# A hybrid decoder step: GpSimd's two-input operations move to VectorE, its scaling of probabilities to ScalarE

## The chip, the cores and the metric

The kernel runs on one core of a Trainium2 chip. The core has five engines with a queue of instructions each, run in order: TensorE (PE in the profile, with PEld for its weight loads), VectorE (DVE), ScalarE (ACT), GpSimd (POOL) and SyncE (SP, which here issues most DMAs). An engine that waits for another one's result holds up everything behind it in its own queue. The metric is the device time of one execution in microseconds: 1519.3 us before the change, the median of three runs (1518.77 to 1519.83).

## The reference

Two layers of a decoder, one step, over a prompt of 512 tokens and eight sequences of eight new tokens with 1024 past positions in a paged cache. All of it is computed in float32.

```
for l in range(2):
    h = rmsnorm(x);  u, z, xbc, dt, cq, ckv, kpe = split(h @ w_in[l])
    A) pooling mixer:  windows of 2/4/8/16 over u, then a small matrix per group
    B) SSD mixer:      xbc = silu(causal_conv4(xbc)); scan in chunks of 128; y * silu(z); rmsnorm
    C) latent attention: q = rmsnorm(cq) @ w_uq; rope; scores on the compressed latent;
                       pr = softmax(scores); pr @ ckv;  w_uv; rmsnorm
    x = x + concat(A, B, C) @ w_out[l]
    x = x + relu(rmsnorm(x) @ w_up[l])**2 @ w_down[l]
y = rmsnorm(x)
```

The new keys, the pooling and convolution histories and the SSD states are returned too.

## The kernel before

The tokens are cut into two chunks, 256 prompt tokens (chunk 0) and 256 prompt tokens with the 64 sample tokens (chunk 1, 320 columns). Activations lie with the features on the partitions and the tokens along the columns. Each large matrix product is made in three passes of a reduced number format (fp32r): a float32 operand is split into a high part, which is a rounded copy, and a low part, which is the difference, and the kernel adds high x high, high x low and low x high (`gemm`, L196 to L203).

The weights of a product of 128 output features come in two halves of 128x512 (`wblock`, L183). For each half SP loads the raw weights (`wr`, 4 buffers), ACT makes the high part (`wh`, L191) and DVE or POOL the low part (`wl`, L192, 3 buffers each). In the FFN (`up`, `down`, with `eng='v'`) DVE makes every low part; in the input projection (`in`), the query projection (`uq`) and the output projection (`out`) POOL makes that of the first half, DVE that of the second. PE needs 12 matmuls, 4 tiles of 128 by 3 passes, for one half.

The mixer of a layer and chunk has several streams: the input projection tile by tile (`w_in`), whose results are taken out by `evac`; the query and key projections; the SSD scan; prompt attention (`prompt_attn`) and, in chunk 1, attention over the paged cache (`sample_attn`); then the output projection. The class `Weave` takes turns between these streams and the FFN of the other chunk, by rates given in `proj` and at the end of the program. This sets the order in which the program is written. A scheduler then sets the order of each engine's queue: it takes instructions by the priority that comes from the place in the program (weight halves are moved 100 places ahead, `evac` 500) and by a time line of its own, so that another engine for an operation can move the instructions around it on all engines.

POOL's other places before the change: in `conv_tile` the product of the convolution's result and its sigmoid (`xa`, L405 and L407); in `evac` the gate `z` times its sigmoid (L479); in `sample_attn` the low part of the rotary keys (`kh` on 32 partitions, L671) and the scaling of one probability tile by its softmax factor (L698); in `prompt_attn` the scaling of each probability tile by the reciprocal of its sum (L581), before PE transposes it. Besides these POOL makes the window sums of the pooling mixer (L436), squares of the first layer's input (L247 to L251), small copies of convolution and pooling histories (L391 to L398, L422 to L429), the state decay of the sample sequences (L886, L890) and two of the final products (L1006). The sigmoid consists of three passes on ACT (L413 to L415) after a clamp on DVE (L412); a convolution is four operations on DVE (L400, L402) with one buffer for its padded input (`XB`).

Of the kernel before, what the change touches and what calls it, by code (L numbers as in the profile page):

```python
# [9 lines left out]
F32 = mybir.dt.float32  # L10
# [3 lines left out]
AF = mybir.ActivationFunctionType  # L14
ALU = mybir.AluOpType
# [74 lines left out]
def step_kernel(ctx: ExitStack, tc: tile.TileContext, I, O):  # L90
    nc = tc.nc
    V, A, G, T, S = nc.vector, nc.scalar, nc.gpsimd, nc.tensor, nc.sync
    E_XA, E_Z, E_KR, E_PR = G, G, G, G

    const = ctx.enter_context(tc.tile_pool(name="const", bufs=1))
    wp = ctx.enter_context(tc.tile_pool(name="wp", bufs=2))
# [5 lines left out]
    def psum(tag, name):  # L102
        tag = {'sp': 'sp' if BANKS['sp'] else 'ac'}.get(tag, tag)
        return psp.tile([P, 512], F32, tag=tag, name=name, bufs=BANKS[tag])
# [70 lines left out]
    def load_raw(src, name, f):  # L175
        t = wp.tile([P, HB, P], F32, tag="wr", name=f"wr_{name}_{f}", bufs=NRAW)
        S.dma_start(t, src[:, f:f + HB])
        return t

    def ahead(n):  # L180
        return tc.high_priority(max(1, min(n, tc.cur_priority - first[0])))

    def wblock(src, name, nk=KT, mw=P, eng=None):  # L183
        halves = []
        with ahead(HP):
            for f in range(0, nk, HB):
                raw = raw0.pop(0) if raw0 else load_raw(src, name, f)
                h = wp.tile([P, HB, P], F32R, tag="wh", name=f"wh_{name}_{f}", bufs=NWH)
                lo = wp.tile([P, HB, P], F32R, tag="wl", name=f"wl_{name}_{f}", bufs=NWL)
                r, hh, ll = raw[:, :, :mw], h[:, :, :mw], lo[:, :, :mw]  # L190
                A.activation(hh, r, AF.Copy)  # L191
                (V if eng == 'v' or (f and eng is None) else G).tensor_tensor(ll, r, hh.bitcast(F32), op=ALU.subtract)  # L192
                halves.append((h, lo))
        return halves

# [152 lines left out]
    def mixer(l, c, mp, ep):  # L348
# [153 lines left out]
        def w_in():  # L502
            for kind in (IN_FILL if l == 0 and c == 1 else IN_ORDER):
                bi = IN_TILES.index(kind)
                mw = 70 if kind == 'kd' else P
                w = wblock(I['w_in'][l, bi], f"in{l}{c}{bi}", mw=mw)
                ps = psum("mm", f"in{l}{c}{bi}")
                gemm(ps, w, ktiles(h_in[c]), cw, mw=mw)
                with ahead(500):
                    evac(kind, ps)  # L510
                if l == 0 and 'masks' in done:
                    load_pages(8)
                done.add(kind)
                yield cw / 96.0
            if smp_c:
                A.dma_start(O['o_stg'][l, :, :STG['p_pool'][0]], stg[:, :STG['p_pool'][0]])
                a_, b_ = STG['p_pool']
                A.dma_start(O['o_stg'][l, :, a_:b_], hist)
                a_, b_ = STG['p_conv']
                A.dma_start(O['o_stg'][l, :, a_:b_], halo)  # L520

        def mla_proj():
            kr, rq = kd[:32], st['rq']
            qT = pp.tile([P, 6, CM], F32, tag="qT", name=f"qT{l}{c}")[:, :, :cw]
            for h0 in (0, 2, 4):
                w = wblock(I['w_uq'][l, :, 2 * h0:2 * h0 + 4], f"uq{l}{c}{h0}", nk=4)
                for h in range(2):
                    ps = psum('mm', f"q{l}{c}{h0 + h}")
                    with tc.issue_after(mark_pe[f"q{l}{c}"]):
                        gemm(ps, w, lambda k: (qhl[:, k], qhl[:, 2 + k]), cw, nk=2, k0=2 * h)  # L530
                    V.tensor_tensor(qT[:, h0 + h], ps[:, :cw], rq, op=ALU.mult)
                    yield 0.75
            st['qT'] = qT
            kt = mp.tile([P, 6, CP], F32, tag=f"kT{c}", name=f"kT{l}{c}")
            vt = mp.tile([P, 2, 384], F32, tag=f"vT{c}", name=f"vT{l}{c}")
            kT[c], vT[c] = kt, vt
            A.activation(kt[64:96], bc(kr[:, :CP], 6), AF.Copy)
            A.activation(kt[96:128], bc(kr[:, :CP], 6), AF.Copy)
            for j in range(3):
                ps = psum("tp", f"kn{l}{c}{j}")  # L540
                T.matmul(ps[:, :CP], uk[:, 2 * j:2 * j + 2], ckvn[:, :CP], start=True, stop=True)
                A.activation(kt[:64, 2 * j], ps[:64, :CP], AF.Copy)
                A.activation(kt[:64, 2 * j + 1], ps[64:, :CP], AF.Copy)
                yield 0.45
            for b in range(2):
                ps = psum("tp", f"v{l}{c}{b}")
                T.matmul(ps[:, :384], ckvn[:, b * P:b * P + P], uv, start=True, stop=True)
                A.activation(vt[:, b], ps[:, :384], AF.Copy)
                yield 0.65
# [8 lines left out]
        def prompt_attn():  # L558
            qT, o = st['qT'], st['o']
            for j in range(3):  # L560
                po = psum('ac', f"o{l}{c}{j}")
                for hh in range(2):
                    h = 2 * j + hh
                    for b in range(2):
                        nb = 2 * c + b + 1
                        nk = nb * P
                        q = qT[:, h, b * P:b * P + P]
                        sc = psum("sc", f"sc{l}{c}{h}{b}")
                        if c == 1:
                            T.matmul(sc[:, :CP], q, kT[0][:, h], start=True, stop=True)  # L570
                            T.matmul(sc[:, CP:nk], q, kT[1][:, h, :nk - CP], start=True, stop=True)
                        else:
                            T.matmul(sc[:, :nk], q, kT[0][:, h, :nk], start=True, stop=True)
                        T.matmul(sc[:, nk - P:nk], idb, matt, start=False, stop=True, skip_group_check=True)
                        nm = mp.tile([P, 4], F32, tag="nm", name=f"nm{l}{c}{h}{b}", bufs=3)
                        V.tensor_reduce(nm[:, 0:1], sc[:, :nk], axis=AX.X, op=ALU.max)
                        V.tensor_scalar(nm[:, 1:2], nm[:, 0:1], -1.0, None, op0=ALU.mult)
                        pr = mp.tile([P, 512], F32, tag="pr", name=f"pr{l}{c}{h}{b}", bufs=NPR)
                        A.activation(pr[:, :nk], sc[:, :nk], AF.Exp, bias=nm[:, 1:2], accum_out=nm[:, 2:3])
                        V.reciprocal(nm[:, 3:4], nm[:, 2:3])  # L580
                        E_PR.tensor_scalar(pr[:, :nk], pr[:, :nk], nm[:, 3:4], 1.0, op0=ALU.mult, op1=ALU.mult)  # L581
                        tp = psum("tp", f"pt{l}{c}{h}{b}")
                        for i in range(nb):
                            T.transpose(tp[:, i * P:i * P + P], pr[:, i * P:i * P + P], idn)
                        pT = mp.tile([P, 512], F32, tag="pT", name=f"pT{l}{c}{h}{b}", bufs=NPT)
                        if b:
                            A.activation(pT[:, :nk], tp[:, :nk], AF.Copy)
                        else:
                            V.tensor_copy(pT[:, :nk], tp[:, :nk])
                        for i in range(nb):  # L590
                            mark_pe[f"pa{l}{c}"] = T.matmul(  # L591
                                po[64 * hh:64 * hh + 64, b * P:b * P + P], vT[i // 2][:, i % 2, h * 64:h * 64 + 64],
                                pT[:, i * P:i * P + P], start=(i == 0), stop=(i == nb - 1)).ins
                        yield 0.55 * nb
                A.activation(o[:, j, :CP], po[:, :CP], AF.Copy)

        def sample_attn():
# [49 lines left out]
            for pq_ in range(NSEQ // 2):  # L647
                nm = mp.tile([P, 15], F32, tag="snm", name=f"snm{l}{c}{pq_}", bufs=2)
                prs = []
# [45 lines left out]
                prn, prs = prs[1], (prs[0], prs[2])  # L695
                V.tensor_scalar(prn, prn, nm[:, 2:3], None, op0=ALU.mult)
                V.tensor_scalar(prs[0], prs[0], nm[:, 0:1], None, op0=ALU.mult)
                G.tensor_scalar(prs[1], prs[1], nm[:, 1:2], 1.0, op0=ALU.mult, op1=ALU.mult)  # L698
                po = psum('sp', f"spo{l}{c}{pq_}")
                tp = psum("tp", f"sptn{l}{c}{pq_}")  # L700
                T.transpose(tp[:CS, :P], prn, idn)
# [24 lines left out]
            for h in range(6):  # L726
                hh, j = h % 2, h // 2
# [532 lines left out]
```

## Time and profile before

| | before |
|---|---|
| time, median of three runs | 1519.3 us |
| time of the profiled execution | 1519.12 us |
| span of the profiled execution | 1517.1 us |
| PE busy | 1426.8 us (94%) |
| DVE busy | 1058.1 us (70%) |
| ACT busy | 829.0 us (55%) |
| POOL busy | 344.4 us (23%) |

The span is the time from the first to the last instruction of the execution; the execution's time is 2.0 us longer. Busy times are those in which an engine has at least one instruction at work; instructions of one engine overlap a little at their ends. A busy PE can still be one whose matmuls stand close together or far apart. The chain of waits goes back from the last instruction to whatever released each instruction, so a share of it is time in which that engine alone held up the end.

### The profile page before, as it was taken

The page shows a single profiled execution, that of the slowest core. Times are in us where ns is not written, and L with a number is a line of the kernel's source. Part 1 is how long each engine was busy: PE and PEld are TensorE (multiplying, and loading weights), DVE is VectorE, ACT ScalarE, POOL GpSimd, SP SyncE. Part 2 cuts the span into 40 slices and gives each one's busy share as a digit, 9 for nine tenths or more (in the row PEclk, how much of TensorE's full clock was granted, in tenths as well). Part 3 has the DMA queues.
Part 4 walks back from the last instruction along what each step waited for, and adds up shares of the span by engine and source line. Part 5 has one row for each costly group of instructions (what it writes and reads, how often), then busy time and mean ns, then how long its engine had stood idle before and what let it go on. Part 6 is the DMA issues. An engine that isn't in the chain of part 4 may idle for free.

```text
span 1517.1 us, 30346 instructions
## 1 busy us (share of the span) xinstructions
PE 1426.8 (94%) x10528; PEld 1358.4 (90%) x10528; DVE 1058.1 (70%) x2201; ACT 829.0 (55%) x1749; POOL 344.4 (23%) x458
## 2 busy tenths in 40 slices
PE   4998987999999969999999999999999998999997
PEld 4877976999999958989999998889989997999997
DVE  6788658876666767866557678886776666655655
ACT  5556535655465655564555565655655564544544
POOL 6365433122200134410110035521241011000000
PEclk8899998999999989999999999999999999999999
DMA  6232424666546633344544453465674454444443
GB/s 207 97 111 74 146 80 138 202 202 199 164 132 188 197 120 95 126 132 142 160 159 152 147 175 108 138 200 172 191 229 144 149 174 127 152 152 148 152 148 109
DMA packets 151995, 228.96 MB, mean 151 GB/s; under 512 B 17826, under 2 KB 60962, under 8 KB 151714
## 3 DMA queue, kind: packets, MB, share of 16 engines
q1 hardware_dynamic: 138178, 216.69, 45.3%
q10 hardware_dynamic: 13664, 10.34, 2.2%
q8 instruction: 83, 1.36, 0.4%
q14 instruction: 70, 0.57, 0.1%
HBM read 219.32 MB, written 7.64 MB: 150 GB/s over the span
## 4 chain that ended last, share of the span: by engine, by line
PE 78%; DVE 11%; DMA 3%; issue 3%; ACT 3%; SPq 1%; POOL 1%; DVEq 0%; ACTq 0%; POOLq 0%
PE up L201 9%; PE up L203 9%; PE up L202 9%; PE dn L203 9%; PE dn L202 9%; PE dn L201 8%; PE out L201 2%; PE out L203 2%; PE out L202 2%; DVE cv L402 2%; PE in L201 2%; PE in L202 2%; PE in L203 2%; PE o L591 2%; PE spo L717 1%
## 5 line engine op out<-in xcount | busy, mean ns | idle before, releaser
L201 PE MATMUL up<-gh_f,wh_up 128*128 128x256 f32 (+1 forms) x1024 | 307.9, 303 | 10.6 <-ACT gh_f L944 8.9
L202 PE MATMUL up<-gl_f,wh_up 128*128 128x256 f32 (+1 forms) x1024 | 309.5, 302 | 2.9 <-DVE gl_f L945 2.3
L203 PE MATMUL up<-gh_f,wl_up 128*128 128x256 f32 (+1 forms) x1024 | 309.4, 303 | 0.0
L203 PE MATMUL dn<-hh,wl_dn 128*128 128x256 f32 (+1 forms) x1024 | 304.7, 298 | 1.1 <-DVE wl_dn L192 0.9
L202 PE MATMUL dn<-hl,wh_dn 128*128 128x256 f32 (+1 forms) x1024 | 304.2, 297 | 0.0
L201 PE MATMUL dn<-hh,wh_dn 128*128 128x256 f32 (+1 forms) x1024 | 303.3, 297 | 0.8 <-ACT wh_dn L191 0.8
L191 ACT ACTIVATE wh_dn<-wr_dn 128x512 fp32r<-128x512 f32 x256 | 160.6, 631 | 179.2 <-PE dn L202 121.6
L191 ACT ACTIVATE wh_up<-wr_up 128x512 fp32r<-128x512 f32 x256 | 160.7, 629 | 151.6 <-PE up L202 100.7
L192 DVE TENSOR_TENSOR wl_dn<-wr_dn,wh_dn 128x512 fp32r<-128x512 f32 x256 | 179.3, 702 | 90.4 <-ACT wh_dn L191 83.0
L192 DVE TENSOR_TENSOR wl_up<-wr_up,wh_up 128x512 fp32r<-128x512 f32 x256 | 181.5, 711 | 86.0 <-ACT wh_up L191 83.3
L201 PEld LDWEIGHTS up<-gh_f,wh_up 128*128 128x128 f32 x1024 | 194.9, 192 | 16.8 <-ACT gh_f L944 11.9
L202 PEld LDWEIGHTS up<-gl_f,wh_up 128*128 128x128 f32 x1024 | 196.1, 192 | 6.7 <-DVE gl_f L945 4.2
L203 PEld LDWEIGHTS up<-gh_f,wl_up 128*128 128x128 f32 x1024 | 196.5, 192 | 3.1 <-issue 0.6
L203 PEld LDWEIGHTS dn<-hh,wl_dn 128*128 128x128 f32 x1024 | 193.6, 189 | 2.6 <-DVE wl_dn L192 1.5
L201 PEld LDWEIGHTS dn<-hh,wh_dn 128*128 128x128 f32 x1024 | 193.6, 189 | 1.4 <-ACT wh_dn L191 1.0
L202 PEld LDWEIGHTS dn<-hl,wh_dn 128*128 128x128 f32 x1024 | 193.4, 189 | 1.3 <-issue 0.7
L201 PE MATMUL in<-gh_h,wh_in 128*128 128x256 f32 (+3 forms) x448 | 137.0, 306 | 9.9 <-ACT gh_h L235 4.9
L203 PE MATMUL in<-gh_h,wl_in 128*128 128x256 f32 (+3 forms) x448 | 137.0, 306 | 2.3 <-DVE wl_in L192 1.3
L202 PE MATMUL in<-gl_h,wh_in 128*128 128x256 f32 (+3 forms) x448 | 135.9, 303 | 2.7 <-DVE gl_h L236 2.7
L192 POOL TENSOR_TENSOR wl_in<-wr_in,wh_in 128x512 fp32r<-128x512 f32 (+1 forms) x55 | 73.9, 1345 | 154.5 <-ACT wh_in L191 149.6
L192 POOL TENSOR_TENSOR wl_out<-wr_out,wh_out 128x512 fp32r<-128x512 f32 x32 | 42.0, 1313 | 268.1 <-ACT wh_out L191 268.1
L671 POOL TENSOR_TENSOR kh<-ku,kh 32x256 fp32r<-32x256 f32 x64 | 58.3, 916 | 168.6 <-ACT kh L669 119.9
(346 smaller groups left out, 2884.7 us busy)
## 6 DMA issues: line engine op xcount, KB each, us to landing
wr_up<-in_w_up SPq DMA_DIRECT2D x256, 256.0 KB, 2.8
wr_dn<-in_w_down SPq DMA_DIRECT2D x256, 256.0 KB, 2.9
wr_in<-in_w_in SPq DMA_DIRECT2D x110, 256.0 KB, 2.8
wr_out<-in_w_out SPq DMA_DIRECT2D x64, 256.0 KB, 2.9
ku<-in_kcache SPq DMA_DIRECT2D x96, 128.0 KB, 2.3
nat<-in_ncache SPq DMA_DIRECT2D x96, 64.0 KB, 2.1
ku<-in_kcache ACTq DMA_DIRECT2D x32, 128.0 KB, 3.2
wr_uq<-in_w_uq SPq DMA_DIRECT2D x12, 256.0 KB, 3.0
```

What stands on the lines that cost most here:

```text
L191: A.activation(hh, r, AF.Copy)
L192: (V if eng == 'v' or (f and eng is None) else G).tensor_tensor(ll, r, hh.bitcast(F32), op=ALU.subtract)
L201: T.matmul(ps[:mw, :cw], wh[:, kk, :mw], ah, start=(k == 0), stop=False)
L202: T.matmul(ps[:mw, :cw], wh[:, kk, :mw], al, start=False, stop=False)
L203: T.matmul(ps[:mw, :cw], wl[:, kk, :mw], ah, start=False, stop=(k == nk - 1))
L402: V.scalar_tensor_tensor(cv[:, :n], X[:, k:k + n], par(l, 'conv_w', m * 4 + k), cv[:, :n], op0=ALU.mult, op1=ALU.add)
L591: mark_pe[f"pa{l}{c}"] = T.matmul(po[64 * hh:64 * hh + 64, b * P:b * P + P], vT[i // 2][:, i % 2, h * 64:h * 64 + 64], pT[:, i * P:i * P + ...
L671: E_KR.tensor_tensor(kh[64:96, :, P:], raw[64:96, :, P:], kh[64:96, :, P:].bitcast(F32), op=ALU.subtract)
L717: mark_pe[f"s{l}{2 * pq_ + 1}"] = T.matmul(po[:, 64 * u:64 * u + NR], nat[:, g], pT[:, o_:o_ + NR], start=False, stop=True, skip_group_che ...
```

## The change

Four places change. The low parts of all weight halves are made by DVE (L192). The three names that chose the engine of the gate products (`E_XA`, `E_Z`) and of the rotary keys' low part (`E_KR`) now mean DVE. The scaling of the probabilities in both attentions, two multiplications in one instruction on POOL, becomes one copy with a scale on ACT (L581, L698). No other line changes, and the arithmetic is the same.

```diff
-    E_XA, E_Z, E_KR, E_PR = G, G, G, G
+    E_XA, E_Z, E_KR = V, V, V
...
-                (V if eng == 'v' or (f and eng is None) else G).tensor_tensor(ll, r, hh.bitcast(F32), op=ALU.subtract)
+                V.tensor_tensor(ll, r, hh.bitcast(F32), op=ALU.subtract)
...
-                        E_PR.tensor_scalar(pr[:, :nk], pr[:, :nk], nm[:, 3:4], 1.0, op0=ALU.mult, op1=ALU.mult)
+                        A.activation(pr[:, :nk], pr[:, :nk], AF.Copy, scale=nm[:, 3:4])
...
-                G.tensor_scalar(prs[1], prs[1], nm[:, 1:2], 1.0, op0=ALU.mult, op1=ALU.mult)
+                A.activation(prs[1], prs[1], AF.Copy, scale=nm[:, 1:2])
```

POOL's queue in the input projection of the first layer's chunk 0, before (`wl_in` are low parts of weight halves, `halo` and `XB` the history copies of the convolution, `xaz` the gate product, `pr` a probability tile):

```order
L192 TENSOR_TENSOR wl_in_0_784<-wr_in_0_781,wh_in_0_783 128x512
L398 COPY halo_194<-XB_672 128x3
L192 TENSOR_TENSOR wl_in_0_920<-wr_in_0_917,wh_in_0_919 128x512
L391 COPY XB_818<-halo_194 128x3
L405 TENSOR_TENSOR xaz_216<-cv_676,se_681 128x256
L581 TENSOR_SCALAR pr_1183<-pr_1183,nm_1180 128x128
L192 TENSOR_TENSOR wl_in_0_1054<-wr_in_0_1051,wh_in_0_1053 128x512
L398 COPY halo_194<-XB_818 128x3
L391 COPY XB_954<-halo_194 128x3
```

The same part of POOL's queue in the changed kernel:

```order
L398 COPY halo_194<-XB_672 128x3
L391 COPY XB_818<-halo_194 128x3
L398 COPY halo_194<-XB_818 128x3
L391 COPY XB_954<-halo_194 128x3
L398 COPY halo_194<-XB_954 128x3
L391 COPY XB_1088<-halo_194 128x3
```

The history copies are left alone there; splits, gate products and scalings have gone from between them.

DVE's queue around the second convolution of that projection, as a difference (`XB` and `cv` are the convolution's input and sum, `nm` the row maximum of a probability tile, `rm` the SSD decay):

```order
 L390 TENSOR_TENSOR XB_818<-in_793,r_in_211 128x256
 L400 TENSOR_SCALAR cv_822<-XB_818,prm_73 128x256
+L192 TENSOR_TENSOR wl_in_0_1054<-wr_in_0_1051,wh_in_0_1053 128x512
+L402 SCALAR_TENSOR_TENSOR cv_822<-XB_818,prm_73,cv_822 128x256
+L405 TENSOR_TENSOR xaz_216<-cv_676,se_681 128x256
 L402 SCALAR_TENSOR_TENSOR cv_822<-XB_818,prm_73,cv_822 128x256 x2
 L192 TENSOR_TENSOR wl_in_4_1060<-wr_in_4_1057,wh_in_4_1059 128x512
-L402 SCALAR_TENSOR_TENSOR cv_822<-XB_818,prm_73,cv_822 128x256
-L854 TENSOR_TENSOR rm_1349<-rb_1342,cst 128x384
 L412 TENSOR_SCALAR cv_822<-cv_822 128x256
```

A split and the gate product of the convolution before stand between the steps of this convolution, and both halves of each weight block are now in this queue.

ACT's queue around the first probability tile of that chunk, as a difference (`wh_in` are high parts of weight halves, L579 the exponential, L581 the scaling, L858 the exponentials of the SSD decay):

```order
 L579 ACTIVATE pr_1183,nm_1180<-sc_1177,nm_1180 128x128
-L548 ACTIVATE vT_906<-v_1045 128x384
-L191 ACTIVATE wh_in_0_1053<-wr_in_0_1051 128x512
-L858 ACTIVATE rm_1334<-rm_1334,ncs_464 128x128 x3
-L191 ACTIVATE wh_in_4_1059<-wr_in_4_1057 128x512
+L191 ACTIVATE wh_in_4_1200<-wr_in_4_1198 128x512
+L858 ACTIVATE rm_1334<-rm_1334,ncs_464 128x128 x2
+L581 ACTIVATE pr_1183<-pr_1183,nm_1180 128x128
+L858 ACTIVATE rm_1334<-rm_1334,ncs_464 128x128
 L548 ACTIVATE vT_906<-v_1048 128x384
```

The scaling stands three instructions behind its exponential, and it waits there for a reciprocal that DVE makes in between.

## Rows read from the trace of the kernel before

**Rows 1.** first lines of the page: span, then busy time by engine

```profile
span 1517.1 us, 30346 instructions
...
PE 1426.8 (94%) x10528; PEld 1358.4 (90%) x10528; DVE 1058.1 (70%) x2201; ACT 829.0 (55%) x1749; POOL 344.4 (23%) x458
```

**Rows 2.** stretches: length, busy us (count) of each engine, clock, DMA share

```profile
40.00:200.00 160.00, 146.30 (x1039) 131.16 (x1039) 127.81 (x307) 94.31 (x231) 80.81 (x113) 0.97 0.33 106
520.00:640.00 120.00, 100.75 (x748) 95.30 (x747) 93.77 (x197) 67.26 (x148) 45.16 (x54) 0.93 0.39 122
880.00:960.00 80.00, 76.39 (x510) 71.19 (x509) 61.89 (x126) 48.55 (x102) 39.82 (x57) 1.00 0.41 130
```

**Rows 3.** the page, part 4: share of the chain that ended last, by engine

```profile
PE 78%; DVE 11%; DMA 3%; issue 3%; ACT 3%; SPq 1%; POOL 1%; DVEq 0%; ACTq 0%; POOLq 0%
```

**Rows 4.** the same chain between 40 and 200 us, by line

```profile
by line: DVE cv L402 7.7%; issue 7.0%; PE in L201 6.3%; PE in L202 6.0%; PE in L203 5.7%; PE out L201 3.4%; DVE wl_in L192 3.4%; PE out L202 3.2%; PE out L203 3.2%; POOL XB L391 1.9%; PE q L201 1.8%; DVE pm L442 1.7%; PE sc L573 1.7%; PE rb
```

**Rows 5.** POOL by line: shapes, count, busy us, mean ns, idle before

```profile
L192 POOL TENSOR_TENSOR wl_in<-wr_in,wh_in 128x512 fp32r<-128x512 f32 (+1 forms) x55 | 73.9, 1345 | 154.5 <-ACT wh_in L191 149.6 <-DVE cq L490 2.3 <-DVE ah L807 2.1
L671 POOL TENSOR_TENSOR kh<-ku,kh 32x256 fp32r<-32x256 f32 x64 | 58.3, 916 | 168.6 <-ACT kh L669 119.9 <-DMA h<-in_state_ssm 22.0 <-issue 20.8
L192 POOL TENSOR_TENSOR wl_out<-wr_out,wh_out 128x512 fp32r<-128x512 f32 x32 | 42.0, 1313 | 268.1 <-ACT wh_out L191 268.1
L581 POOL TENSOR_SCALAR pr<-pr,nm 128x128 f32<-128x128 f32 (+3 forms) x48 | 27.6, 577 | 127.7 <-DVE nm L580 115.9 <-DVE qlh L630 2.9 <-DVE qll L631 2.9
L405 POOL TENSOR_TENSOR xaz<-cv,se 128x256 f32<-128x256 f32 x20 | 17.2, 859 | 13.4 <-ACT se L415 13.4
L192 POOL TENSOR_TENSOR wl_uq<-wr_uq,wh_uq 128x512 fp32r<-128x512 f32 x12 | 16.1, 1347 | 43.5 <-ACT wh_uq L191 41.4 <-ACT dec L816 2.0
...
L479 POOL TENSOR_TENSOR xaz<-xaz,sz 128x256 f32<-128x256 f32 (+1 forms) x12 | 11.6, 966 | 3.7 <-ACT sz L415 3.6
...
L698 POOL TENSOR_SCALAR spr<-spr,snm 128x512 f32<-128x512 f32 x8 | 8.0, 1000 | 49.7 <-DVE snm L694 29.0 <-DMA ku<-in_kcache 6.1 <-PE o L591 5.9
```

**Rows 6.** DVE by line and shape

```profile
L192 DVE TENSOR_TENSOR wl_dn<-wr_dn,wh_dn 128x512 fp32r<-128x512 f32 x256 | 179.3, 702 | 90.4 <-ACT wh_dn L191 83.0 <-PE dn L203 3.3
L192 DVE TENSOR_TENSOR wl_in<-wr_in,wh_in 128x512 fp32r<-128x512 f32 x51 | 39.4, 773 | 13.0 <-ACT wh_in L191 9.1 <-POOL wl_in L192 2.1 <-PE in L202 1.6
L670 DVE TENSOR_TENSOR kl<-ku,kh 128x256 fp32r<-128x256 f32 x64 | 37.8, 597 | 21.7 <-ACT kh L669 20.6 <-DMA nat<-in_ncache 0.6
...
L999 DVE TENSOR_TENSOR hl<-fr,hh 128x256 fp32r<-128x256 f32 x64 | 27.8, 436 | 0.9
L402 DVE SCALAR_TENSOR_TENSOR cv<-XB,prm,cv 128x344 f32<-128x344 f32 x30 | 24.4, 812 | 0.6
...
L402 DVE SCALAR_TENSOR_TENSOR cv<-XB,prm,cv 128x256 f32<-128x256 f32 x30 | 22.1, 736 | 0.6
...
L466 DVE TENSOR_TENSOR kd<-in,cr 32x256 f32<-32x256 f32 x2 | 0.8, 405 | 0.0
```

**Rows 7.** timeline, 60 to 67 us: start, duration, engine, line, operation

```profile
60.61 1.28 POOL L192 TENSOR_TENSOR wl_in<-wr_in,wh_in 128x512 fp32r<-128x512 f32 x1 [0.29 <-ACT wh_in L191]
60.72 1.31 DVE L400 TENSOR_SCALAR cv<-XB,prm 128x256 f32<-128x256 f32 x1
...
65.77 0.41 DVE L400 TENSOR_SCALAR cv<-XB,prm 128x256 f32<-128x256 f32 x1
...
66.22 0.49 DVE L402 SCALAR_TENSOR_TENSOR cv<-XB,prm,cv 128x256 f32<-128x256 f32 x1
```

**Rows 8.** ACT by line and shape

```profile
L579 ACT ACTIVATE pr<-sc,nm 128x512 f32<-128x512 f32 x12 | 8.2, 687 | 16.6 <-DVE nm L577 8.0 <-PE pt L584 3.7 <-DVE qlh L630 2.6
...
L579 ACT ACTIVATE pr<-sc,nm 128x128 f32<-128x128 f32 x12 | 4.4, 364 | 2.2 <-DVE nm L577 1.5 <-DVE nm L580 0.3 <-PE pt L584 0.2
```

**Rows 9.** PE's waits: who waited for whom, us, times, longest

```profile
PE ss_q L215 <- DVE acc_q L227: 30.3, 2, 15.2
```

**Rows 10.** POOL's waits between 40 and 200 us

```profile
POOL pr L581 <- DVE nm L580: 9.9, 5, 3.9
```

## The prediction

> **What bounds the kernel now.** I read the first lines of the page, then busy time by stretch, then the chain of waits, then the groups of each engine. The first lines show TensorE (PE) busy for 1426.8 of 1517.1 us and VectorE (DVE) for 70% [rows 1]. The execution took 1519.12 us, 2.0 around its span, and the median of the runs shown is 1519.3, so I work from 1519.1. TensorE's idle time is not spread evenly. Three stretches that hold input projections, convolutions and gates show 146.3 of 160, 100.75 of 120 and 76.39 of 80 us: 36.6 us idle in 360. There DVE is busy for 127.81, 93.77 and 61.89, that is 283.5 us or 79%, and GpSimd (POOL) for 165.8 of its 344.4 us [rows 1, 2]. The chain goes through PE for 78% of the span, through DVE for 11% (167 us), ACT 3% (45 us) and POOL 1% (15 us) [rows 3]. Elsewhere PE is its own bound; I put DVE's 167 us into some 500 us of mixer work, start and hand-overs, where they are about a third of the time. So the change is worth what it does to DVE's queue in those 500 us, and 30 us of PE's wait there, two waits for a sum of squares behind a row of DVE splits [rows 9], stay: these splits are not touched and the order around them is the same.
>
> **What goes from POOL.** Weight splits 73.9 + 42.0 + 16.1, rope differences 58.3, gates 17.2 + 11.6, scalings 27.6 + 8.0: 254.7 us in the groups shown, 74% of POOL's busy time [rows 1, 5]. POOL is not full, so its own time is worth only the part on the chain: 15 us, 3.0 of them the small copy POOL XB L391 between 40 and 200 us (1.9% of 160) [rows 3, 4]. A split takes 0.702 us on DVE where POOL is quiet against 1.345, a gate about 0.436 against 0.859 [rows 5, 6], and the copies no longer stand behind a 1.3 us split, as the rows of POOL's order show. I take 8 of the 15 us as gained, between 4 and 13.
>
> **What DVE gets back.** DVE is held while POOL works. The same 128x256 operation of L400 took 1.31 us beside a split on POOL that ran from 60.61 to 61.89, and 0.41 with POOL idle; L402 took 0.49 alone [rows 7]. Over all its instances L402 means 0.736 and, for 344 columns, 0.812, where 0.49 and at most 0.66 (0.49 x 344/256) would be expected: 30 x 0.246 + 30 x 0.152 = 12 us lost. DVE's own splits of w_in lose 51 x 0.071 = 3.6, kl 64 x (0.597 - 0.436) = 10.3, taking a full-width row of as many columns as its price alone [rows 6]. L402 and wl_in lose 15.6 of 85.9 us, 18%. On DVE's 167 us of the chain that is 30 us, and 74% of POOL's work goes: 22 us gained. The low end is L402's 12 us, x 0.74 = 9; the high end 35, if it is the long, held instances that form the chain, since one held instance lost 0.90 of 1.31.
>
> The Trainium skill, SBUF — State Buffer, section "Who interferes with whom", has it harder: the port pair that the two engines share is locked by whichever instruction starts first, for its whole length, and the other one stops. By that rule nearly all of POOL's time beside a DVE that is busy 79% would be DVE's loss, and the sum would come out as in the first rival below. The row at 60.72 agrees with it, a split that loses 0.071 us on average does not.
>
> **What DVE gets.** 99 splits x 0.702 = 69.5 us, 20 + 12 gates x 0.436 = 14, 64 rope differences x 0.405 (32x256, nearest row) = 26 [rows 5, 6]. The rope differences run beside page reads and FFN matmuls, where PE hides them, and kl gives back 10.3 there; I cost them at nothing. Without that cover they would add 26 - 10 = 16 us. Of the other 84 us, 67 splits (47 us) and the gates (14 us) belong to the three stretches and their like: 61 us. DVE stood on the chain for a third of that time, so I charge a third, 20 us; the 23 us of w_out's splits stand beside steady matmuls, 2 us: 22 in all. The low end is 8, with the 21% of the time that DVE is idle in the stretches used first; the high end is 40, from two thirds. A gate now waits on DVE for ACT's sigmoid, and the next tile's L402 and the next splits stand behind it; POOL waited 13.4 us for that [rows 5], but the new order puts a convolution step in between, and the high end holds it.
>
> **What ACT gets.** 48 scalings at the price of the exponentials of the same shapes, 0.364 to 0.687, mean 0.53, and 8 at 0.687: 25 + 5.5 = 31 us [rows 8]. ACT's 45 us of the chain are 9% of the 500 us, so 3 us. Each scaling waits for a reciprocal in DVE's queue, and behind it on ACT stand the exponentials of the decay and the next weight halves, for which PE waits. POOL waited for that reciprocal 9.9 us in five waits, up to 3.9, between 40 and 200 us [rows 10]. The new order has 1 to 3 other ACT instructions ahead of the scaling, which covers most of it; 0 to 10 us, I take it as in the 3.
>
> **Sum.** -8 - 22 + 22 + 3 = -5: 1519.1 - 5 = 1514. That is a small rest of large terms, so its sign is not safe.
>
> **Rivals.** A, the lock gives back more: if the held instances are the chain, 35 instead of 22 and 13 instead of 8 come back, -48 + 25 = -23 at the far end and -18 with part of it, 1501. For it: the row at 60.72 [rows 7]. Against: the mean loss of a DVE split is 0.07 us [rows 6]. By the rule of the SBUF page it would be this case.
>
> B, DVE becomes the bound, slower. Place: the input projections. There PE uses a half of weights in 12 matmuls, and each half now asks 0.70 us of DVE, where every second one did. DVE goes from 283.5 to about 283.5 + 61 - 38 = 306 of 360 us (38 is 18% x 74% of 283.5). If splits stand in its in-order queue behind the convolution steps, the chain is on DVE for two thirds of that time: 84 x 0.5 = 42 is paid, -30 + 42 + 3 = +15, 1534. It decides from a half upwards. For it: DVE's load, and L402 is the largest item of the chain [rows 4]. Against: a fifth of DVE's time there is free.
>
> C, ACT's new waits. 56 scalings held by 0.2 us each with the weight halves behind are 11 us, +6 in all, 1525. For it: waits of up to 3.9 us [rows 10]; against: ACT is busy only 55%.
>
> D, no change: the terms meet within 3 us, or PE's two long waits [rows 9] and its own work are the bound whatever DVE does, 1519.
>
> **How the numbers follow.** Three us, 0.2%, is about what these runs can tell from no change. Forecast (3 to 15 faster) 0.33, A 0.14: faster 0.47. D 0.20. B 0.25 and C 0.08: slower 0.33. The range is 1498 to 1534: from A's 1501 less a little to B's price; the forecast alone would be 1504 to 1516. The likeliest time is 1514.
>
> **What would show it.** L402 at 0.49 and about 0.6 us and kl near 0.43: the lock is gone. Splits on DVE at 0.70 us. DVE busy near 1120 us, 1058 + 110 - 48. ACT near 860. POOL near 90. DVE's share of the chain unchanged near 11% and POOL's gone would bear the forecast out; a DVE share of 14% and more, with PE waiting for wl_in or for DVE's convolution, would be B; ACT idle before L581 with PE waiting for weight halves would be C. The forecast is wrong if PE's idle time in the first 280 us grows, or if either long wait for the sum of squares goes away.

## The result and the profile after

The changed kernel took 1500.38 us (median of four runs, 1497.12 to 1510.85) where the kernel before took 1519.03 on the same chip. The ratio is 0.989, with a 95% interval of 0.9861 to 0.9919: 12 to 21 us faster, where 5 were forecast. The difference of the medians, 18.7 us, is a little more than the ratio gives, 17, because the ratio goes by all runs of both kernels.

The profiled run was the slowest of the four, 1510.85 us. A second profile of the same program, that of the first experiment below, took 1497.08. The lines of this section come from the first profile. Over the whole span PE is idle for 90.3 us in the kernel before, 78.5 in the first profile and 76.5 in the second, so 12 to 14 us of the gain are idle time of PE that went away, in both.

The two profiles of the one program differ in the clock that TensorE was granted. The same 40 us in both, first the slower profile, then the faster (columns as in [rows 2], with the clock behind the last bracket):

```profile
960.00:1000.00 40.00, 40.00 (x321) 33.34 (x320) 27.93 (x69) 16.66 (x40) 9.30 (x12) 0.74 0.46 143
960.00:1000.00 40.00, 39.99 (x388) 35.95 (x388) 35.12 (x80) 23.43 (x54) 9.81 (x12) 1.00 0.52 166
```

PE is busy throughout in both and works at 321 matmuls in one, 388 in the other. From 978 to 998 us the clock of the slower profile was 0.50, the lower of its two levels, after 38 us of busy PE at 1.00. Over the whole span the clock was 0.968 in the run of 1510.85 us and 0.977 in the fastest of the eight runs of this program, 1494.96. So a difference of some ten us between two runs can be the clock alone. The gain is not: on the chip of the experiments the median clock was 0.973 in the kernel before and 0.974 in the changed one.

The first lines of the page and the chain's shares by engine, changed kernel, answer to [rows 1, 3]:

```profile
span 1509.1 us, 30143 instructions
...
PE 1430.6 (95%) x10528; PEld 1363.7 (90%) x10528; DVE 1071.3 (71%) x2407; ACT 855.7 (57%) x1805; POOL 86.5 (6%) x196
...
PE 84%; DVE 7%; ACT 4%; DMA 3%; issue 2%; SPq 1%; ACTq 0%; DVEq 0%
```

VectorE (DVE) has 206 instructions more and only 13 us more of busy time. Its share of the chain falls from 11% to 7%, where the prediction had it unchanged, and GpSimd (POOL) is no longer on it. TensorE (PE) takes the place: 84% instead of 78%.

The three stretches of [rows 2], changed kernel, same columns:

```profile
40.00:200.00 160.00, 149.70 (x1054) 134.71 (x1053) 130.31 (x362) 99.53 (x244) 16.07 (x48) 0.95 0.34 106
520.00:640.00 120.00, 105.41 (x782) 100.02 (x781) 98.00 (x238) 73.01 (x162) 10.62 (x29) 0.94 0.40 125
880.00:960.00 80.00, 79.99 (x558) 74.78 (x556) 69.54 (x173) 50.91 (x111) 15.69 (x38) 1.00 0.41 130
```

PE is idle for 24.9 of these 360 us, where it was 36.6. DVE is busy for 297.9 of them, 83%, and PE still waits less: how full DVE is did not decide. The stretches are fixed in time, so those of the faster kernel hold a little more of the program.

The chain between 40 and 200 us by line, changed kernel, answers to [rows 4]:

```profile
by line: PE in L201 11.2%; PE in L202 10.6%; PE in L203 10.2%; PE out L203 4.7%; PE out L201 4.6%; PE out L202 4.4%; issue 3.8%; PE rb L847 3.4%; DVE wl_in L192 3.4%; PE y L871 1.9%; ACT wh_in L191 1.7%; PE o L591 1.6%; PE q L201 1.4%; PE y
```

Before, the convolution step L402 headed this list with 7.7% of 160 us, 12.3 us. Now it is not among the lines shown, the last of which have 1.4%. The input projection's matmuls stand in front, with 32% where they had 18%.

DVE's groups, changed kernel, answer to [rows 6]; the columns are those of that group:

```profile
L192 DVE TENSOR_TENSOR wl_in<-wr_in,wh_in 128x512 fp32r<-128x512 f32 x102 | 70.0, 687 | 11.1 <-ACT wh_in L191 10.0
L670 DVE TENSOR_TENSOR kl<-ku,kh 128x256 fp32r<-128x256 f32 x64 | 27.0, 421 | 14.1 <-ACT kh L669 13.7
L671 DVE TENSOR_TENSOR kh<-ku,kh 32x256 fp32r<-32x256 f32 x64 | 26.7, 417 | 1.8
L402 DVE SCALAR_TENSOR_TENSOR cv<-XB,prm,cv 128x344 f32<-128x344 f32 x30 | 17.2, 573 | 0.4
L402 DVE SCALAR_TENSOR_TENSOR cv<-XB,prm,cv 128x256 f32<-128x256 f32 x30 | 14.3, 478 | 0.1
L405 DVE TENSOR_TENSOR xaz<-cv,se 128x256 f32<-128x256 f32 x20 | 8.8, 440 | 0.6 <-ACT se L415 0.5
```

Every price of DVE came down to that of an undisturbed instruction: w_in's splits from 773 to 687 ns, kl from 597 to 421, L402 from 812 and 736 to 573 and 478. That a few instances make the difference is seen in the rows of L402 alone (minimum, median, maximum in ns over both shapes; first the kernel before, then the changed one):

```profile
L402 DVE SCALAR_TENSOR_TENSOR cv<-XB,prm,cv x60: 467/577/1650, 54.6 to 947.7; 128x256 f32<-128x256 f32 x30, 128x344 f32<-128x344 f32 x30
```

```profile
L402 DVE SCALAR_TENSOR_TENSOR cv<-XB,prm,cv x60: 466/523/579, 51.8 to 933.4; 128x256 f32<-128x256 f32 x30, 128x344 f32<-128x344 f32 x30
```

Taken by shape, the medians hardly move, from 485 to 478 ns and from 577 to 573; the longest instance lost 1.07 us. Two instances in the timeline of the kernel before (start, duration), beside two splits on POOL:

```profile
78.02 1.59 POOL L192 TENSOR_TENSOR wl_in<-wr_in,wh_in 128x512 fp32r<-128x512 f32 x1
78.50 1.38 DVE L402 SCALAR_TENSOR_TENSOR cv<-XB,prm,cv 128x256 f32<-128x256 f32 x1
80.15 0.47 DVE L402 SCALAR_TENSOR_TENSOR cv<-XB,prm,cv 128x256 f32<-128x256 f32 x1
80.40 1.37 POOL L192 TENSOR_TENSOR wl_in<-wr_in,wh_in 128x512 fp32r<-128x512 f32 x1 [0.79 <-ACT wh_in L191]
```

The step at 78.50 began while the split was running, and it ended at 79.88, 0.27 us after the split. The step at 80.15 began before its split and took no longer than an undisturbed one. The 60 instances bear this out. 21 took more than 0.7 us, and each of them began while a split or a gate product was running on POOL (one within 3 ns of its start). Fourteen began beside a split, and each ended 0.28 us (256 columns) or 0.37 to 0.38 us (344 columns) after it. Seven others began 0.06 to 0.42 us ahead of a split or gate product, and none of these is longer by 10 ns. It holds for DVE's other two-input instructions too. Against the median of the same group in the second profile, the 249 that began while a two-input operation ran on POOL are 87 us longer in sum; the 101 that began ahead of one are 2.8 us longer.

ACT's scalings, changed kernel, answer to [rows 8, 10] (after the bar: busy us, mean ns, then its idle time before them and who ended it):

```profile
L581 ACT ACTIVATE pr<-pr,nm 128x512 f32<-128x512 f32 x12 | 8.6, 719 | 0.5 <-DVE nm L580 0.5
L581 ACT ACTIVATE pr<-pr,nm 128x384 f32<-128x384 f32 x12 | 7.3, 610 | 2.0 <-DVE nm L580 2.0
...
L698 ACT ACTIVATE spr<-spr,snm 128x512 f32<-128x512 f32 x8 | 5.7, 716 | 0.8 <-DVE snm L694 0.8
```

ACT waits 3.3 us in all for the reciprocals of these three groups. PE's two long waits for a sum of squares, [rows 9], stay as forecast:

```profile
PE ss_q L215 <- DVE acc_q L227: 28.3, 2, 15.3
```

### The profile page after: what moved, and what is told of

Same layout as the page of the kernel before. It is cut to its first block, busy times and chain, and to the rows that moved or that the text cites. A ratio compares the mean times of both kernels' runs of the same rounds, so it can differ in the third digit from the quotient of the medians.

```text
span 1509.1 us, 30143 instructions
## 1 busy us (share of the span) xinstructions
PE 1430.6 (95%) x10528; PEld 1363.7 (90%) x10528; DVE 1071.3 (71%) x2407; ACT 855.7 (57%) x1805; POOL 86.5 (6%) x196
## 4 chain that ended last, share of the span: by engine, by line
PE 84%; DVE 7%; ACT 4%; DMA 3%; issue 2%; SPq 1%; ACTq 0%; DVEq 0%
PE up L201 9%; PE up L203 9%; PE dn L203 9%; PE dn L202 9%; PE up L202 9%; PE dn L201 9%; PE in L201 3%; PE in L202 3%; PE in L203 3%; PE out L201 2%; PE out L203 2%; PE out L202 2%; PE o L591 2%; PE spo L717 2%; DMA wr_dn<-in_w_down 1%
## 5 line engine op out<-in xcount | busy, mean ns | idle before, releaser
L192 DVE TENSOR_TENSOR wl_up<-wr_up,wh_up 128x512 fp32r<-128x512 f32 x256 | 177.5, 695 | 94.6 <-ACT wh_up L191 82.6
L192 DVE TENSOR_TENSOR wl_dn<-wr_dn,wh_dn 128x512 fp32r<-128x512 f32 x256 | 176.0, 691 | 93.8 <-ACT wh_dn L191 90.0
L191 ACT ACTIVATE wh_in<-wr_in 128x512 fp32r<-128x512 f32 (+1 forms) x110 | 67.3, 615 | 66.2 <-PE in L202 39.5
L201 PEld LDWEIGHTS in<-gh_h,wh_in 128*128 128x128 f32 (+1 forms) x448 | 85.0, 190 | 10.4 <-ACT gh_h L235 5.2
L202 PEld LDWEIGHTS in<-gl_h,wh_in 128*128 128x128 f32 (+1 forms) x448 | 84.8, 189 | 3.7 <-DVE gl_h L236 2.5
```

The source lines that it names most:

```text
L192: V.tensor_tensor(ll, r, hh.bitcast(F32), op=ALU.subtract)
L201: T.matmul(ps[:mw, :cw], wh[:, kk, :mw], ah, start=(k == 0), stop=False)
L202: T.matmul(ps[:mw, :cw], wh[:, kk, :mw], al, start=False, stop=False)
```

## The experiments

Two theories stood against each other first. By one the gain is VectorE's time, which GpSimd's two-input work beside it had lengthened. By the other it is GpSimd's own slow results on the path. The letters in the expectations are short names for these and their parts. Every time is compared with the kernel before on the same chip, 1516 to 1518 us there. A ratio is given with its 95% interval, a gain in us is worked out from the ratio, and "over the changed kernel" is the difference of two ratios, times 1517 us; its uncertainty is the root of the sum of the squares of both half-widths.

### The changed kernel again

> The changed kernel once more, on the chip on which its parts run. 1500 us (1497 to 1505), ratio 0.985 to 0.991. In the first profile VectorE's chain share fell from 11% to 7%; it should show 7% again, with PE idle less in the stretches of the input projections.

Measured: 1496.92 us, 0.9873 (0.9858 to 0.9888), 19.2 us faster. The first ratio, 0.989, agrees. I summed the durations of all DVE instructions in both traces: 1147.7 us before, 1169.9 here. The groups that got the moved work rose by 107 us (splits 63, rope differences 27, gates 17), and the sum of all rose by only 22: the other groups are 85 us shorter. Busy time rose less, 13 us, because it counts overlapping ends once.

### Only the weight splits

```diff
-                (V if eng == 'v' or (f and eng is None) else G).tensor_tensor(ll, r, hh.bitcast(F32), op=ALU.subtract)
+                V.tensor_tensor(ll, r, hh.bitcast(F32), op=ALU.subtract)
```

> Only the weight splits go to VectorE (132 us of GpSimd's 255). Theory L (VectorE gets back the time for which GpSimd's reads hold it): the gain follows the GpSimd time removed less the VectorE work added, so about half of 19 us, 1508 to 1512. Theory P (a split takes 0.70 us instead of 1.35 on its way to TensorE, and GpSimd's queue no longer delays it): nearly all, 1500 to 1505.

Measured: 1506.39 us, 0.9946 (0.9926 to 0.9967), 8.2 us faster. The time lies between the ranges of the two theories and decides for neither. The chain between 40 and 200 us:

```profile
by line: PE in L201 13.4%; PE in L203 13.3%; PE in L202 13.1%; PE out L203 4.7%; PE out L201 4.6%; PE out L202 4.5%; PE rb L847 3.3%; issue 3.3%; PE y L871 2.5%; PE sc L573 2.1%; PE o L591 1.8%; PE q L201 1.4%; PE px L832 1.4%; DVE wl_in L1
```

L402 has left these lines here too, with the rope differences, gates and scalings still on POOL. So it stood there in the main because of POOL's splits, by what they took from DVE or by their late ends.

### Gates with rope, rope alone, gates alone

The first of the three; the second sets only `E_KR` to `V`, the third only `E_XA` and `E_Z`:

```diff
-    E_XA, E_Z, E_KR, E_PR = G, G, G, G
+    E_XA, E_Z, E_KR, E_PR = V, V, V, G
```

> Only gate products and rope differences go to VectorE (about 93 us of GpSimd's time). Theory L: 5 to 7 us faster, 1512 to 1514. Theory P: the splits still take 1.35 us on GpSimd, at most 2 us faster, 1517 to 1519.

> Only the low part of the rotary keys (64 operations of 0.92 us on GpSimd) goes to VectorE. The prediction costed this at nothing. Theory F (while GpSimd works on a page it keeps the page's buffer, the next page read waits in SyncE's queue, and weight loads wait behind it; the shared key split kl is held too): nearly all that gates and rope differences gained together, 1509 to 1512, gained in the two stretches of the paged attention. Theory G (the gates were what counted): 1514 to 1517.

> The kernel before with only the gate products (L405, L479) on VectorE; rope differences, splits and scaling stay on GpSimd. Theory G (the gates carry what gates and rope gave together, 6 us): 1509 to 1512 where the kernel before is 1516. Theory R (it takes both, since the rope differences alone gave nothing and GpSimd's queue holds the gates back only together with them): 1513 to 1517.

Measured: gates with rope 1509.32 us, 0.9958 (0.9943 to 0.9974), 6.4 us faster; rope alone 1515.19, 0.9994 (0.9982 to 1.0006), no change; gates alone 1514.68, 0.9979 (0.9965 to 0.9993), 3.2 us faster. The single ones make 4.1 of the 6.4, which the intervals allow, so neither theory of the last expectation is excluded. Gates with rope gain more than theory P allowed, at most 2 us. The chain between 40 and 200 us with gates and rope moved, then with rope alone:

```profile
by line: PE in L203 9.8%; PE in L202 9.6%; PE in L201 9.5%; DVE cv L402 6.4%; issue 4.0%; PE out L201 3.5%; PE out L203 3.3%; PE out L202 3.3%; DVE wl_in L192 2.8%; PE sc L573 2.2%; PE y L871 2.0%; PE q L201 1.8%; DVE cv L400 1.7%; PE rb L8
```

```profile
by line: DVE cv L402 7.7%; issue 7.1%; PE in L201 6.2%; PE in L202 6.0%; PE in L203 5.7%; PE out L201 3.5%; DVE wl_in L192 3.4%; PE out L202 3.3%; PE out L203 3.2%; POOL XB L391 1.9%; PE q L201 1.8%; DVE pm L442 1.7%; PE sc L573 1.7%; ACT r
```

Rope alone leaves this chain as it was, L402 in front and POOL's copy XB L391 in the list. The gates take the copy out of it, and most of L402 stays. I also summed L402's pieces of the chain over the whole span: 27.3 us before, 25.2 with rope moved, 11.8 with the gates, 13.5 with both, 4.8 with the splits, 4.2 in the changed kernel.

### Only the scalings on ACT

```diff
-                        E_PR.tensor_scalar(pr[:, :nk], pr[:, :nk], nm[:, 3:4], 1.0, op0=ALU.mult, op1=ALU.mult)
+                        A.activation(pr[:, :nk], pr[:, :nk], AF.Copy, scale=nm[:, 3:4])
```

and the same at L698, `A.activation` in place of `G.tensor_scalar`.

> Only the scaling of probabilities goes to ScalarE (36 us of GpSimd's time, nothing added to VectorE). Theory L: 3 to 5 us faster, 1514 to 1516, since VectorE is held less. Theory P: no change, 1518 to 1520. If ScalarE's new waits count (rival C of the prediction), 2 us or more slower.

Measured: 1516.42 us, 0.9999 (0.9985 to 1.0013). Alone it gives nothing. L402 has 35.0 us of the chain here, more than before at the same time: when it leaves the chain, another line may follow close behind, so a sum of the chain is no price.

### GpSimd's reads put back, with nobody waiting for them

The changed kernel, with two subtractions on POOL after each split that POOL made before; their result is not read. In this kernel and the next two the lines below L116 have numbers higher by 1 to 5.

```diff
+                if not (eng == 'v' or (f and eng is None)):
+                    for i in range(2):
+                        a, b = (h[:, 2 * i + k, :min(mw, 88)].bitcast(F32) for k in range(2))
+                        G.tensor_tensor(shadow[:, :min(mw, 88)], a, b, op=ALU.subtract)
```

> The changed kernel, and on GpSimd, for each of the 100 halves that it split before, two subtractions of 128x88 elements between parts of the high half, whose result nobody reads: GpSimd is as busy as before with reads of SBUF, but nothing waits for it. Theory L (VectorE held by GpSimd's reads): much of the splits' gain is lost again, since VectorE now has the splits and the holding, 1503 to 1512, and L402 goes back over 0.6 us. Theory P (latency on GpSimd): 1495 to 1500.

Measured: 1501.45 us, 0.9894 (0.9873 to 0.9914), 3.2 us over the changed kernel, plus or minus 3.8. The added groups, as the page of lines shows them:

```profile
L197 POOL TENSOR_TENSOR shadow<-wh_in 128x88 f32<-128x88 f32 x104 | 67.0, 644 | 173.3 <-ACT wh_in L192 166.5 <-ACT tot L824 2.6
L197 POOL TENSOR_TENSOR shadow<-wh_out 128x88 f32<-128x88 f32 x64 | 41.4, 647 | 520.8 <-ACT wh_out L192 518.3
L197 POOL TENSOR_TENSOR shadow<-wh_uq 128x88 f32<-128x88 f32 x24 | 13.4, 558 | 50.5 <-ACT wh_uq L192 49.6
```

These 121.8 us of POOL lengthened DVE's instructions by 12.7 us (sum of durations 1182.6), 0.10 us for each us of POOL. The 255 us of the kernel before had cost 85, 0.33 each. So the dose was a seventh of what the change took away, and the run can't tell the two theories apart. It says only that POOL being busy is not by itself what costs DVE: what POOL does counts, since nine tenths of this time ran beside a busy DVE.

### More work in VectorE's queue

The changed kernel, with a reduction on DVE after each of those splits; its result is not read.

```diff
+                if not (eng == 'v' or (f and eng is None)):
+                    V.tensor_reduce(shadow[:, :1], hh.bitcast(F32), axis=AX.XY, op=ALU.max)
```

> The changed kernel, and on VectorE a maximum over each of those 100 high halves, some 0.6 to 0.7 us each, whose result nobody reads: the added work of the splits doubled. If VectorE's added work costs a third of its length, as the prediction charged, 18 to 24 us slower than the changed kernel, 1515 to 1521. If VectorE's idle time covers it, 0 to 8 us slower, 1497 to 1505.

Measured: 1547.52 us, 1.0203 (1.0183 to 1.0223), 50 us over the changed kernel, for 100 instructions of 0.68 us or less. That seemed to say that DVE's work costs three quarters of its length. The chain early in this run says otherwise; pieces between 28 and 52 us, then the same transfer in the changed kernel:

```profile
43.56 0.26 SPq L164
44.12 0.27 SPq L164
44.69 0.26 SPq L164
45.25 0.26 SPq L164
45.81 0.26 SPq L164
46.37 5.31 DMA x_in<-in_x
```

```profile
20.09 8.41 DMA x_in<-in_x
```

The load of the second chunk's input starts 26 us later. L164 there reads page numbers into SyncE's registers, one every 0.56 us. In the changed kernel SyncE's queue has all of these reads behind that load; here 40 stand ahead of it. PE's first product of the queries was 22 us late by that. The edit doesn't touch them; the scheduler, whose time line the added work changes, set this order. So some 22 of the 50 us came with the order and not with DVE's work.

The next run takes that away: the same reductions, but only from the seventeenth such split on, with the load ahead of the page reads again.

> The changed kernel with a VectorE reduction of 128x512 (0.677 us in the run before this one, result unread) over the halves that GpSimd split before, from the seventeenth such half on: 84 instead of 100, 57 us of added VectorE work. In the run with all 100, SyncE's queue had 40 page-number reads ahead of the load of x_in, and PE was 22 us late by the first q product; here x_in's load stands ahead of the page reads, as in the changed kernel. Theory V (VectorE's work in that queue costs about half its length, and 22 of the 50 us were SyncE's order): +25 to +32 us over the changed kernel, 1522 to 1529 where the kernel before is 1516. Theory T (a third of its length, as the prediction charged): +19, 1516. Theory W (the 50 us were all VectorE's work, the late x_in only its first form): +42, 1539.

Measured: 1522.75 us, 1.0029 (1.0011 to 1.0048), 23.7 us over the changed kernel, plus or minus 3.6. The largest of the added groups:

```profile
L197 DVE TENSOR_REDUCE shadow<-wh_in 128x1 f32<-128x512 f32 x40 | 27.2, 679 | 0.0
...
L197 DVE TENSOR_REDUCE shadow<-wh_out 128x1 f32<-128x512 f32 x32 | 21.7, 679 | 0.0
```

84 x 0.679 = 57 us were added, so a us of DVE's work in this queue costs 0.42 us, 0.35 to 0.48. That lies between the third that the prediction charged and the half of the new theory; the three quarters fell. In the profiles of this run and of the first experiment PE is idle for 14.5 us more and busy for 11.6 us more, at a granted clock of 0.967 against 0.975, so nearly half of this price shows as a slower PE and not as a wait.

### The changed kernel with one part back, or one more part gone

From the changed kernel, the scalings (L581 here, and L698) go back to POOL:

```diff
-                        A.activation(pr[:, :nk], pr[:, :nk], AF.Copy, scale=nm[:, 3:4])
+                        G.tensor_scalar(pr[:, :nk], pr[:, :nk], nm[:, 3:4], 1.0, op0=ALU.mult, op1=ALU.mult)
```

> The changed kernel with the two scalings (L581, L698) back on GpSimd. Alone the scalings gave 0, the splits 8 to 10 us and gates with rope 6 to 7; the whole change 19. Theory A (the parts add up, and the scaling gives the missing 4 us once the rest of GpSimd's work is gone): 1501 to 1503 where the kernel before is 1516. Theory I (splits and gates give more together than apart, the scaling gives nothing still): 1497 to 1499.

The rope differences go back to POOL:

```diff
-    E_XA, E_Z, E_KR = V, V, V
+    E_XA, E_Z, E_KR = V, V, G
```

> The changed kernel with the rope differences (L671, 64 of them, 58 us of GpSimd) back on GpSimd. They overlap VectorE's cache splits (L670), which went from 645 to 421 ns each when they left. Theory H (PE hides this stretch, the prediction's reading): 1496 to 1499 where the kernel before is 1516, within 2 us of the changed kernel. Theory L (VectorE's time that GpSimd takes counts wherever it is lost): about 20 us of VectorE's time lost again at half its length, 1505 to 1508.

More leaves POOL: the window sums (shown), the state decay, the squares of the first layer's input and the last of POOL's products, to DVE or ACT:

```diff
-                G.tensor_tensor(e[:, lo:], prev[:, lo:], prev[:, lo - sh:-sh], op=ALU.add)
+                V.tensor_tensor(e[:, lo:], prev[:, lo:], prev[:, lo - sh:-sh], op=ALU.add)
```

> The changed kernel with the rest of GpSimd's arithmetic moved too: window sums, state decay and final products to VectorE, squares of the first input and the state selection to ScalarE; memsets and small copies stay. Theory L: VectorE is still held for some 20 us, most of it in the first 40 us beside the squares; 2 to 6 us faster than the changed kernel, 1491 to 1495. If VectorE's load counts more than its holding, no gain or 1 to 4 us slower, 1497 to 1501.

Measured: scalings back 1506.80 us, 0.9915 (0.9891 to 0.9940); rope back 1501.31, 0.9881 (0.9854 to 0.9908); more gone 1499.31, 0.9907 (0.9881 to 0.9933). With the scalings back the kernel is 6.4 us over the changed one, plus or minus 4.4, and gains 12.9 us where splits (8.2) and gates with rope (6.4) make 14.6: these parts add up. That the scalings are worth the 6.4 us is not shown. Between the profiles of this run and of the first experiment PE's idle time hardly differs, 75.0 and 76.5 us; its busy time is 10.4 us longer, at a clock of 0.968 against 0.975, and the changed kernel itself ran at 0.968, in 1510.85 us. The rope differences are worth nothing here as they were alone, although their groups show 10 us of DVE's time lost again (421 to 585 ns):

```profile
L670 DVE TENSOR_TENSOR kl<-ku,kh 128x256 fp32r<-128x256 f32 x64 | 37.2, 585 | 21.1 <-ACT kh L669 20.8
...
L671 POOL TENSOR_TENSOR kh<-ku,kh 32x256 fp32r<-32x256 f32 x64 | 56.7, 889 | 264.8 <-ACT kh L669 174.1 <-DMA ku<-in_kcache 29.9 <-PE up L202 29.9
```

Taking more from POOL brings no gain: by the ratios it is 5.2 us over the changed kernel, plus or minus 4.6, where theory L had 2 to 6 us faster. No version here beats the changed kernel.

## Why the prediction came out as it did

**Right sign, a quarter of the size.** The forecast was -5 us, measured were -18.7 (-17 by the ratio) and -19.2. The range held the time only because it reached as far as rival A, whose 1501 us it is; A had a chance of 0.14, and 3 to 15 us faster had 0.33. In the sum two terms of 22 cancel, so that the sign came out right is in part luck.

**What goes from POOL (-8, 4 to 13).** POOL left the chain, as the step said: 1% before, 17 us by its pieces, not listed now. Its worth was not measured apart.

**What DVE gets back (-22, 9 to 35): too small in its amount.** It took the mean loss of L402 and of w_in's splits, 18%, and spread it over DVE's 167 us of the chain. Two things were wrong in it. The amount: 48 us of DVE's lengthening were to come back, and 85 did. And the mean: the loss is not spread. Of the 21 long instances of L402, 15 stood on the chain, and 11.6 of L402's 27.3 us there were lengthening. All its instances in the program shortened by 15 us, 30 x 0.239 + 30 x 0.258. Its part of the chain fell by 23, from 27.3 to 4.2, but that is more than came back: the rest is time in which L402 takes no longer than it does now, and other work has its place on the chain. The same comparison for all of DVE, each instruction against the median of its group in the second profile, gives 40.5 us of lengthening on the chain before and 11.1 after. So some 29 us of it left the chain, within the bounds and nearer the high end; the run with only the scalings moved has 49.3 at the time of the kernel before, so this sum is good to some ten us and is no price. The prediction had held instances on the chain as the term's high end and as rival A's condition, "if the held instances are the chain". The row at 60.72 [rows 7] was the better witness, the mean of the splits the worse one. The row at 66.22, which the prediction read as L402 alone, ran 0.24 us beside the split that began at 66.47; it began first and was not lengthened, so the 0.49 us are right. The run with the splits alone moved agrees: 4.8 us of the chain were left to L402.

The instances show the rule that the prediction took from the Trainium skill, SBUF — State Buffer, "Who interferes with whom": whichever of the two engines starts first has the shared ports for its whole instruction, and the other one waits. The prediction's reading of it, that nearly all of POOL's time beside a busy DVE would be lost, does not follow. By the same section a DVE instruction comes under the rule only if it takes two inputs from SBUF or runs in a 2-port mode, and where DVE starts first it is POOL that waits. The trace agrees: the six splits that began while L402 was running took 1.37 to 1.68 us, where the one of [rows 7] took 1.28. Here 255 us of POOL cost DVE 85 us.

**What DVE gets (+22, 8 to 40).** 84 us at a third; measured at 0.42, with 0.35 to 0.48, which is 35. By that price it was too low by 13, and within its bounds; but the reductions are other work than the splits and gates, and their price holds some of the clock. The rope differences were costed at nothing, and were nothing in both runs that moved them alone; the 10.3 us that kl would give back came back.

**What ACT gets (+3, 0 to 10).** Moved alone, 0, within 2 us. The waits for the reciprocals that rival C needed were 3.3 us in the groups shown. ACT is busy for 855.7 us, as forecast (860).

**The sum again.** With one price of 0.42 for the time that DVE gets and gives, the terms are -8, -75 x 0.42 = -31 (85 less the 10 of kl, which are hidden), +35 and 0, together -4. With all 15 us of POOL on the chain they would be -11. The measured 17 to 19 is more than either. The lengthening that left the chain, 29 us, is no more than the 31 of this sum, so it does not close the gap. The gap would close if the moved work cost less than the reductions did, or if the time given back counted for more than its length. No run put a price on either by itself, so which term is off stays open.

**The rivals.** B fell: DVE is busy for 83% of the three stretches, and its share of the chain went down. C fell: the scalings alone cost nothing, within 2 us. D fell: PE's long waits stayed, and its other idle time went from 36.6 to 24.9 us.

**What stays open.** How the 19 us divide between DVE's held instructions and POOL's late results; what the moved work costs by itself; whether the scalings are worth anything; and why the clock fell in one profile and not in the other.

## What to carry to other kernels

Where one engine slows another, look at the single instances, which of the two began first, and whether the chain goes through the held ones: with medians longer by 4 and 7 ns, single steps of up to 1.65 us stood on the chain. Work that moves to the engine that was held can cost less than it gives back. What it costs depends on the place: the reductions beside the projections cost 0.42 us per us, the rope differences beside page reads nothing that two runs could tell. When two runs differ by some ten us, compare the granted clock first. When a probe adds work to a scheduled program, see first whether the order of the DMA queue has stayed the same.

## What was not expected of the hardware

- A two-input DVE instruction is held by POOL only if POOL's began first: 87 us of lengthening in 249 instances, against 2.8 us in the 101 that DVE began first. A held convolution step ends 0.28 or 0.37 us after POOL's split.
- What POOL costs DVE depends on its instruction: 0.33 us per us for the mix of the kernel before, 0.10 for subtractions of 128x88.
- A difference over 32 partitions takes DVE as long as one over 128: 417 ns for 32x256 (L671), 421 for 128x256 (L670).
- A scaled copy on ACT is dearer than the exponential of the same tile, 719 ns for 128x512 against 687 [rows 8], though behind each exponential of L579 stands a read of its sum, of 0.20 us.
- SyncE needs 0.56 us for each page number that it reads into a register, and the load that came to stand behind 40 of them started 26 us later.
